# A norm's scale and offset both made on GpSimd, and the sample norm's parameter loads held until their tile's GELU, in an eight-core encoder trunk

## The chip, the cores and the metric

The kernel runs on all 8 cores of one Trainium2 chip. Each core works on its own part of the tokens and its span is measured on the device. The metric is the device time of the slowest core, in microseconds (us). The cores form two dies (cores 0 to 3 and cores 4 to 7).

Every execution lists the span of each core and its mean granted TensorE clock (1.0 is full speed). The program has two states. In the fast state all cores show a clock of about 0.996 and the program takes about 5100 us. In the slow state the cores of one die, sometimes of both, are granted less and the program takes from about 5190 to over 6000 us. The mean hides the form: on core 6 of the profiled run before, the clock was 0.81 from 25 to 385 us and 1.00 from 390 to 5130 us.

The rule that calls a run fast still lets in runs with a die at 0.986 to 0.991, which take 5136 to 5161 us. So I also quote "clean" runs: fast ones in which both dies have a clock (the median of their cores) of at least 0.995.

## The reference, cut to what matters

The model is a four-layer encoder trunk. Each layer is FFN, mixer, FFN, each with a residual and a LayerNorm. The change touches one norm inside the mixer, that of `v` in the spatial gating unit:

```python
# group B: gMLP spatial gating unit
z = jax.nn.gelu(h[..., 2 * D_CONV:], approximate=False)
u = z[..., :D_SGU]
v = layer_norm(z[..., D_SGU:], sgu_ln_g, sgu_ln_b)
s = u * sgu_mix(v, w_sgu, b_sgu)
# layer_norm: (x - mean) * rsqrt(var + 1e-5) * gain + offset, over the last axis (512 here)
...
return x, buf[:, -CONV_CTX:], v      # v of the sample streams is an output of its own
```

The normalised `v` of the sample streams (16 streams, 64 new frames each) is an output, so for these rows the kernel must also apply the norm's gain and offset explicitly. For all other rows they are folded into later operations.

## The kernel before: the parts that matter

The kernel writes down all operations of a half of the work with their dependencies and a planned duration (`dur`, in ns). A list scheduler (`schedule`) then simulates them and fixes in which order each engine issues them. Two consequences: a changed `dur` or dependency can reorder everything that comes after it, and an engine that waits at one entry of its list holds up all entries behind it.

A core does two halves; the sample rows sit in the last of three column groups of the second half. The norm of `v` handles up to four tiles of 128 tokens at once, so its statistics are arrays of 128 x 2 to 4 elements:

```python
def part_v(g, wv):
    ...
    for j, (v0, kk, t0, o0, on, smp) in enumerate(ts):
        op("pe", mm, ...)                                                   # L1018  v = x @ w_in
        op("act", ... activation(func=AF.Gelu) ..., kind="vg")              # L1023
        op("dve", ... bn_stats ..., kind="bn")                              # L1026
    ...                                                                     # L1031  bn_aggr: mean, variance
    Y, A = 36, 40
    op("dve", ... S(Y) = variance + EPS ..., dur=70)                        # L1040
    op("pool", ... S(Y) = S(Y) ** -0.5 ..., dur=900, port=True)             # L1042  scale
    op("dve", lambda e: e.scalar_tensor_tensor(out=S(A), in0=M2(0), scalar=-1.0, in1=S(Y),
              op0=ALU.mult, op1=ALU.mult), reads=[st], writes=[st], dur=70) # L1044  offset = -mean*scale
    for j, (...) in enumerate(ts):
        if not smp:
            op("act", ... activation(Identity, scale=Y[j], bias=A[j]) ...)  # L1054  v scaling (ScalarE)
            continue
        op("dve", ... (z - mean) * Y[j] ...)                                # L1059
        op("act", ... copy ...)                                             # L1063
        for hf in range(2):
            op("sp", ... dma_start(out=gb, in_=sgu_ln gain, broadcast to 128 partitions) ...)    # L1067
            op("sp", ... dma_start(out=be, in_=sgu_ln offset, broadcast to 128 partitions) ...)  # L1071
            op("dve", ... vo = z * gb ...)                                  # L1075
            op("pool", ... vo = vo + be ...)                                # L1078
            op("sp", ... dma_start(out=sgv_d[l], in_=vo) ...)
```

Everything issued with `"sp"` goes through one DMA queue, in list order. The same queue carries the shift copies of the depthwise convolution (L983 and L988), up to 32 per column group. They copy the convolution input into shifted positions, and the convolution's matmuls (L1119) need them:

```python
def part_a4(g):
    for s in range(4):
        for i in range(4):
            op("sp", ... dma_start(out=A4v[32*s:32*s+32, i, :, 0:wdt], in_=ABF[...]) ..., sem="a4")   # L983
            if smp:
                op("sp", ... dma_start(out=A4v[...], in_=ABF[...]) ..., sem="a4")                     # L988
```

Other lines in the profiles: L783 and L814 are the FFN's matmuls, L1177 the spatial mix (it reads the scaled `v`), L1230 the output projection, L604 the additions that prepare a LayerNorm's sums (on GpSimd and DVE), L654 and L677 the matmuls that finish those sums.

## Time and profile before

| | Time (us) | Note |
|---|---|---|
| 4 runs | 5103.65, 5105.04, 5728.84, 6049.52 | the first two fast, the others slow |
| Profiled run, a fifth | 5161.06 | called fast; die of cores 4 to 7 at 0.986 |
| Median of three | 5728.84 | a slow run |
| Core 2 in the profiled run | 5094.0 | clock 0.996 |
| Core 6 in the profiled run (slowest) | 5159.5 | clock 0.982 |

The page gives for each engine its busy time, its share of the span and its instructions. These are the engines of the slowest core before:

```profile
PE 5090.7 (99%) x34514; PEld 3093.9 (60%) x34514; DVE 2552.7 (49%) x5095; ACT 1850.6 (36%) x3513; POOL 1152.2 (22%) x1347
```

TensorE (PE) is busy 99% of the time. Nothing but TensorE work, its clock or its few waits can move the total; every other engine has slack on average. Core 6 had a lower clock in that execution, so from here on core 2 is read, which was undisturbed.

The list of TensorE's waits, core 2, before. Each line says which matmul waited, for which engine's or DMA's result, how long in all, how many times, and the longest:

```profile
PE psall L783 <- DMA ring<-w_all: 16.1, 1, 16.1
PE psall L1177 <- ACT ss L1054: 9.7, 5, 2.4
PE psall L677 <- DVE fr L675: 7.7, 4, 6.6
...
PE psall L1119 <- DMA sa<-abf: 1.5, 2, 0.8
```

The first line is the start of the kernel, when the first weights arrive. The second is what the change aims at: the spatial mix waits for the scaled `v`, up to 2.4 us at a time. The last: the convolution hardly waits for its shift copies.

The timeline of core 2 shows one of these waits (start, length, engine, line, operation, output<-input; in brackets the idle time of that engine before and what ended it):

```profile
3467.17 1.26 POOL L1042 TENSOR_TENSOR stat<-stat,nhalf 128x4 f32<-128x4 f32 x1
3468.42 0.99 POOL L604 TENSOR_TENSOR ss<-ss,X 128x384 f32<-128x384 f32 x1
3468.47 3.69 DVE L1044 SCALAR_TENSOR_TENSOR stat<-stat 128x4 f32<-128x4 f32 x1 [0.40 <-POOL stat L1042]
3469.38 0.98 POOL L604 TENSOR_TENSOR ss<-ss 128x384 f32<-128x384 f32 x1
3470.33 0.85 POOL L604 TENSOR_TENSOR ss<-ss,X 128x384 f32<-128x384 f32 x1
3471.15 0.98 POOL L604 TENSOR_TENSOR ss<-ss 128x384 f32<-128x384 f32 x1
3472.19 1.45 ACT L1054 ACTIVATE ss<-psall,stat 128x512 bf16<-128x512 f32 x2 [2.95 <-DVE stat L1044]
3474.91 0.43 PE L1177 MATMUL psall<-wt,ss 128*64 128x128 bf16 x6 [2.37 <-ACT ss L1054]
3476.98 3.99 PE L783 MATMUL psall<-XT,ring 128*128 128x384 bf16 x16
```

The offset takes 162 ns in the median of a core's 24 such instructions, which are of two to four columns. Here it takes 3.69 us, as do all four instructions of four columns on core 2. It begins within 0.05 us of the first of four back-to-back GpSimd additions and ends when the last of them ends. ScalarE has waited 2.95 us for it, and TensorE 2.37 us for ScalarE. The reason is in the table by windows (busy time of each engine, the granted clock, the DMA share and rate; core 2, before), of 20 us and of the dip inside them:

```profile
3472.00:3492.00 20.00, 17.64 (x121) 10.47 (x119) 16.44 (x38) 11.36 (x20) 15.50 (x16) 0.91 0.48 97
3476.10:3479.50 3.40, 3.40 (x20) 1.73 (x19) 2.63 (x8) 2.96 (x5) 3.40 (x4) 0.50 0.25 80
```

TensorE is busy all but the 2.36 us of its wait, but the clock granted over these 20 us is only 0.91: it falls to half for 3.41 us and is full otherwise. That is another 1.7 us (half of 3.41) that no list of waits shows.

### The profile page before, as it was taken

What the parts mean: (1) busy time and instruction counts of PE and PEld (TensorE: products, weight loads), DVE (VectorE), ACT (ScalarE), POOL (GpSimd) and SP (SyncE); (2) the same over time, 40 slices, a digit from 0 to 9 for tenths busy, and PEclk for the clock granted to TensorE, in tenths of its full rate; (3) what the DMA queues carried; (4) which work ended last, traced back from release to release, by engine and by line L of the source; (5) the groups of instructions that cost most, each with busy time, mean ns of one, the idle gap of its engine ahead of it and who ended that gap; (6) DMA issues with size and microseconds to landing.
All of it is one profiled execution on the core that took longest, in us unless ns stands there. A gap on an engine that the chain in (4) does not pass through costs nothing.

```text
span 5159.5 us, 86449 instructions; the slowest of 8 cores (5094.0 to 5159.5 us)
## 1 busy us (share of the span) xinstructions
PE 5090.7 (99%) x34514; PEld 3093.9 (60%) x34514; DVE 2552.7 (49%) x5095; ACT 1850.6 (36%) x3513; POOL 1152.2 (22%) x1347
## 2 busy tenths in 40 slices
PE   8999999999999999999999999999999999999998
PEld 4555666666666666666555555555555555555556
DVE  1267262672537553672527725267262682626736
ACT  1136131461326332461315513146131462313623
POOL 2014120141203311141202402015120151111410
PEclk8889999999999999999999999999999999999999
DMA  9334544345535545446834445344544445444451
GB/s 155 50 59 79 88 71 66 62 78 89 84 54 98 93 70 84 71 76 109 161 58 85 81 74 78 62 74 76 89 70 66 67 86 83 62 74 70 76 85 48
DMA packets 269208, 407.73 MB, mean 79 GB/s; under 512 B 33168, under 2 KB 107024, under 8 KB 268816
## 3 DMA queue, kind: packets, MB, share of 16 engines
q0 software_dynamic: 181360, 334.66, 41.6%
q1 hardware_dynamic: 87456, 67.54, 5.4%
q8 instruction: 284, 4.65, 0.4%
q14 instruction: 108, 0.88, 0.1%
HBM read 684.79 MB, written 11.47 MB: 135 GB/s over the span
## 4 chain that ended last, share of the span: by engine, by line
PE 94%; DVE 3%; ACT 1%; DMA 1%; SPq 1%; issue 0%; POOL 0%; ACTq 0%; DVEq 0%; POOLq 0%
PE psall L783 52%; PE psall L814 26%; PE psall L926 4%; PE psall L1230 3%; PE psall L1018 2%; PE psall L1119 2%; PE psall L1097 2%; SPq L983 1%; DVE X L726 1%; DVE ss L604 0%; DVE X L730 0%; DMA XT<-xin 0%; PE psall L1177 0%; PE psall L677 0%; PE psall L654 0%
## 5 line engine op out<-in xcount | busy, mean ns | idle before, releaser
L783 PE MATMUL psall<-XT,ring 128*128 128x384 bf16 (+3 forms) x16896 | 2757.8, 326 | 20.9 <-DMA ring<-w_all 18.2
L783 PEld LDWEIGHTS psall<-XT,ring 128*128 128x128 bf16 x16896 | 1657.8, 98 | 1105.1 <-issue 34.3
L789 ACT ACTIVATE ss<-psall 128x384 f32<-128x384 f32 (+3 forms) x1056 | 508.9, 484 | 1943.5 <-PE psall L783 1942.2
L814 PE MATMUL psall<-ss,ring 128*128 128x384 bf16 (+5 forms) x6272 | 1066.8, 323 | 0.0
L797 DVE TENSOR_TENSOR ss<-ss,psall 128x384 bf16<-128x384 f32 (+3 forms) x768 | 416.1, 547 | 1260.3 <-PE psall L783 1234.5
L585 POOL DMA_DIRECT2D ring<-w_all x623 | 449.3, 723 | 2312.6 <-PE psall L783 2019.1
L814 PEld LDWEIGHTS psall<-ss,ring 128*128 128x128 bf16 x6272 | 611.7, 98 | 382.8 <-issue 1.6
L613 ACT ACTIVATE ss<-X,sbi 128x384 f32<-128x384 f32 (+5 forms) x584 | 335.4, 600 | 700.7 <-DVE X L746 700.6
L746 DVE SCALAR_TENSOR_TENSOR X<-X,sg,psall 128x384 f32<-128x384 f32 (+5 forms) x584 | 342.3, 603 | 404.5 <-PE psall L814 394.7
L604 POOL TENSOR_TENSOR ss<-ss 128x384 f32<-128x384 f32 (+3 forms) x262 | 258.8, 988 | 1002.2 <-ACT ss L613 852.3
L797 DVE TENSOR_TENSOR sa<-ss,psall 128x384 bf16<-128x384 f32 (+3 forms) x288 | 157.7, 548 | 589.1 <-PE psall L783 589.1
L814 PE MATMUL psall<-sa,ring 128*128 128x384 bf16 (+5 forms) x2352 | 438.1, 323 | 0.0
L740 ACT ACTIVATE XT<-X,pars 128x384 bf16<-128x384 f32 (+3 forms) x528 | 320.1, 689 | 93.2 <-DVE X L730 93.0
L726 DVE SCALAR_TENSOR_TENSOR X<-X,sbi,psall 128x384 f32<-128x384 f32 (+5 forms) x584 | 333.6, 597 | 4.4 <-ACT ss L689 3.7
L814 PEld LDWEIGHTS psall<-sa,ring 128*128 128x128 bf16 x2352 | 230.5, 98 | 143.5
L604 DVE TENSOR_TENSOR ss<-ss 128x384 f32<-128x384 f32 (+5 forms) x393 | 239.9, 615 | 112.3 <-ACT ss L1133 64.6
L1230 PE MATMUL psall<-ss,ring 128*128 128x384 bf16 (+3 forms) x1536 | 253.3, 324 | 6.6 <-ACT ss L1158 5.7
L926 PE MATMUL psall<-XT,ring 128*128 128x384 bf16 (+4 forms) x1536 | 257.9, 327 | 0.1
L730 DVE TENSOR_TENSOR X<-X,psall 128x384 f32<-128x384 f32 (+4 forms) x512 | 237.4, 543 | 0.1
L1230 PEld LDWEIGHTS psall<-ss,ring 128*128 128x128 bf16 x1536 | 148.1, 98 | 105.9 <-issue 16.9
L926 PEld LDWEIGHTS psall<-XT,ring 128*128 128x128 bf16 x1536 | 149.1, 98 | 100.2 <-issue 1.5
L699 ACT ACTIVATE ss<-ss 128x384 f32<-128x384 f32 (+4 forms) x194 | 99.3, 512 | 221.9 <-DVE ss L694 113.5
(115 smaller groups left out, 2933.8 us busy)
## 6 DMA issues: line engine op xcount, KB each, us to landing
ring<-w_all POOLq DMA_DIRECT2D x623, 512.0 KB, 7.0
sa<-abf SPq DMA_DIRECT2D x204, 103.0 KB, 2.3
sa<-abf SPq DMA_DIRECT2D x68, 102.8 KB, 2.4
X<-xin SPq DMA_DIRECT2D x4, 1536.0 KB, 32.3
y<-X SPq DMA_DIRECT2D x8, 768.0 KB, 9.3
sa<-abf SPq DMA_DIRECT2D x60, 78.5 KB, 2.2
X<-xin SPq DMA_DIRECT2D x2, 1656.0 KB, 21.8
XT<-xin POOLq DMA_DIRECT2D x4, 768.0 KB, 17.7
```

The costliest lines, as they stand in the source:

```text
L585: op("pool", lambda e: e.dma_start(out=RING[t.slot][:].rearrange("p (h n) -> p h n", h=2), in_=w_d[u].rearrange("h p n -> p h n")), writes ...
L604: op(eng, lambda e: e.tensor_tensor(out=self.sa(o), in0=a[0](), in1=b[0](), op=ALU.add), reads=[a[1], b[1]], writes=[o], dur=d_pool(n) if ...
L613: op("act", lambda e: e.activation(out=self.sa(sq), in_=src(), func=AF.Square, **kw), reads=rd, writes=[sq], dur=d_act(n, 1 if sqb is not ...
L726: op("dve", lambda e, k=k: e.scalar_tensor_tensor(out=xs(k), in0=xs(k), scalar=SBI[:, q, k:k + 1], in1=PS[:, m.slot, 0:n], op0=ALU.add, op ...
L740: op("act", lambda e, k=k: e.activation(out=XT[:, k, c0:c1], in_=xs(k), func=AF.Identity, scale=lg[:, k:k + 1], bias=lb[:, k:k + 1]), read ...
L746: op("dve", lambda e: e.scalar_tensor_tensor(out=X[:, k, c0:c1], in0=X[:, k, c0:c1], scalar=SG[:, q, k:k + 1], in1=PS[:, bank.slot, 0:n], ...
L783: ins = e.matmul(PS[:, bank.slot, 0:n], lhsT=RING[w.slot][:, h * 1024 + k * 128:h * 1024 + (k + 1) * 128], rhs=XT[:, k, c0:c1], start=(k = ...
L789: op("act", lambda e, bg=bg, sil=sil, n=n: e.activation(out=SS[sil.slot][:, 0:n], in_=PS[:, bg.slot, 0:n], func=AF.Silu), reads=[bg], writ ...
L797: return e.tensor_tensor(out=gap(gts)[:, o0:o0 + n], in0=SS[sil.slot][:, 0:n], in1=PS[:, bu.slot, 0:n], op=ALU.mult)
L814: ins = e.matmul(PS[:, y.slot, 0:n], lhsT=RING[wd[b // 16].slot][:, (b % 16) * 128:(b % 16 + 1) * 128], rhs=gap(gt[g][f // 2])[:, o0:o0 + ...
L926: ins = e.matmul(PS[:, bank.slot, 0:n], lhsT=RING[wa[c].slot][:, h * 1024 + k * 128:h * 1024 + (k + 1) * 128], rhs=XT[:, k, c0:c1], start= ...
L1230: ins = e.matmul(PS[:, y.slot, 0:n], lhsT=RING[wo[d // 2].slot][:, o0:o0 + 128], rhs=SS[src.slot][:].bitcast(BF16)[:, (k % 2) * GW:(k % 2) ...
```

## The change

The intent is twofold. The offset moves to GpSimd, right behind the scale, so that the chain loses one crossing between engines and the stalled DVE instruction disappears. And the gain and offset loads of the sample norm wait for their tile's GELU, so that they do not occupy work buffers for most of a layer.

```diff
+                    vgi.append(len(G.ops) - 1)           # the GELU of tile j
 ...
-                op("dve", ... S(Y) = variance + EPS ..., dur=70)
+                def ynm(e):
+                    e.tensor_scalar(out=S(Y), in0=M2(1), scalar1=EPS, scalar2=None, op0=ALU.add)
+                    return e.tensor_scalar(out=S(NM), in0=M2(0), scalar1=-1.0, scalar2=None, op0=ALU.mult)
+                ynm.multi = True
+                op("dve", ynm, reads=[st], writes=[st], dur=140)
                 op("pool", lambda e: e.tensor_tensor(out=S(Y), in0=S(Y), in1=NHALF[:, 0:nt], op=ALU.pow),
-                   reads=[st, tONE], writes=[st], dur=900, port=True)
-                op("dve", lambda e: e.scalar_tensor_tensor(out=S(A), in0=M2(0), scalar=-1.0, in1=S(Y), op0=ALU.mult,
-                                                           op1=ALU.mult), reads=[st], writes=[st], dur=70)
+                   reads=[st, tONE], writes=[st], dur=1200, port=True)
+                op("pool", lambda e: e.tensor_tensor(out=S(A), in0=S(NM), in1=S(Y), op=ALU.mult), reads=[st], writes=[st],
+                   dur=150, port=True)
 ...
                            writes=[be], dur=650, dma=400, sem="sgb%d%d" % (l, hf))
+                        for o in G.ops[-2:]:             # the gain load and the offset load
+                            o.after.add(vgi[j])
```

More of the change, by code (lines that the diff above doesn't have):

```diff
@@ L1010, in part_v @@
                 st = Tile("st", "st")
-                vbs, zs = [], []
+                vbs, zs, vgi = [], [], []
                 for j, (v0, kk, t0, o0, on, smp) in enumerate(ts):
@@ L1036, in S @@
                     return STAT[st.slot][:, a:a + b]
-                Y, A = 36, 40
+                Y, A, NM = 36, 40, 44
                 def M2(b):
                     return STAT[st.slot][:, 24:24 + 2 * nt].rearrange("p (a b) -> p a b", b=2)[:, :, b]
-                op("dve", lambda e: e.tensor_scalar(out=S(Y), in0=M2(1), scalar1=EPS, scalar2=None, op0=ALU.add),
-                   reads=[st], writes=[st], dur=70)
+                def ynm(e):
[3 more added lines that the diff above has]
+                op("dve", ynm, reads=[st], writes=[st], dur=140)
                 op("pool", lambda e: e.tensor_tensor(out=S(Y), in0=S(Y), in1=NHALF[:, 0:nt], op=ALU.pow),
-                   reads=[st, tONE], writes=[st], dur=900, port=True)
-                op("dve", lambda e: e.scalar_tensor_tensor(out=S(A), in0=M2(0), scalar=-1.0, in1=S(Y), op0=ALU.mult,
-                                                           op1=ALU.mult), reads=[st], writes=[st], dur=70)
+                   reads=[st, tONE], writes=[st], dur=1200, port=True)
+                op("pool", lambda e: e.tensor_tensor(out=S(A), in0=S(NM), in1=S(Y), op=ALU.mult), reads=[st], writes=[st],
+                   dur=150, port=True)
                 for j, (v0, kk, t0, o0, on, smp) in enumerate(ts):
```

## The prediction

> **What bounds the kernel.** TensorE. The page's first part gives it 5090.7 us busy of a 5159.5 us span (99%), the chain of work that ended last is 94% TensorE, and the cores' list shows granted clocks of 0.98 to 1.00. By stretches, TensorE idles 19 us before 30 us, 18.5 us after 5130 us, and only 31 us (0.6%) in between; that is all there is to win.
>
> **What the change removes, adds and moves.**
> - DVE: out goes the scalar_tensor_tensor for the offset, 24 times, median 162 ns; in comes a tensor_scalar of the same size.
> - GpSimd: 24 more multiplications on 2 to 4 elements. The pow on the same tiles takes 876 ns and a 256-column addition 732 ns; my estimate from these is 0.2 to 0.5 us each, on an engine 22% busy.
> - One crossing between engines goes: DVE, GpSimd, DVE, ScalarE becomes DVE, GpSimd, ScalarE.
> - The eight gain and eight offset loads of the sample norm move. The timeline of the DMA queue shows them running far ahead: three at 2 to 3 us, used at 2881 us; the others at 2711, 3367, 4025 and 4684 us. So three or four of the 30 work buffers are held nearly throughout.
>
> **How much is critical.** In the list of waits TensorE waits for the v norm's scaling 4 times, 7.3 us in all, 2.2 us the longest. The timeline shows why: in the second half's layers 1 to 3 the small offset instruction on DVE takes 3.7 us instead of 0.16, and ends just as four back-to-back GpSimd additions end. The Trainium skill, "SBUF — State Buffer", section "SBUF: two separate sides", says that a DVE instruction with two SBUF inputs and a GpSimd one exclude each other for a whole instruction; this trace agrees (3.69 to 3.70 us, three times). The new GpSimd multiplication at worst queues behind one 1 us addition. I expect 5 to 7 us from it.
>
> The parameter loads: DVE needs them about 20 us after the GELU, and they land in 3.4 us, so nobody should wait. Four issues of 0.43 us may fall among the 32 shift copies of the last group and push these by up to 2 us per layer (TensorE waits for such copies 4.1 us now). The freed buffers matter little: hardly any TensorE wait is for buffers. The order is recomputed from changed durations, so other waits will shift by some us.
>
> **Prediction.** The ratio of fast runs is 0.999: 5098 us in the fast state against 5103.65, with 5075 to 5125 for fast runs alone. A median of three may be a slow run, as 5728.84 was; the recorded range, 5075 to 5760, allows for that, not for an effect of the change. Chances on fast runs: faster by over 2% 0.02, within 2% 0.96, slower 0.02.
>
> **What would show it.** The 3.7 us DVE instruction is gone; TensorE's wait for the v scaling falls from 7.3 to under 2 us; GpSimd gains 24 short instructions; the parameter loads sit at about 2855, 3515, 4170 and 4830 us; TensorE's busy time is unchanged within 0.5% at equal clock.
>
> **What would make it wrong.** The new order starves the shift copies or a LayerNorm chain, so that TensorE's idle time grows by more than 20 us; parameter loads arrive late and hold up DVE; a difference of clock is taken for one of the change.

## The result, and the profile after

Ratios here are the mean time of one kernel's fast runs over that of the other's fast runs of the same rounds, so they are not quite the ratio of the medians that I quote.

| | Fast runs (us) | Slow runs (us) |
|---|---|---|
| before | 5103.65, 5105.04 | 5728.84, 6049.52 |
| after | 5099.83, 5099.93, 5100.05, 5100.81 | 5430.03 |

The ratio of fast runs is 0.9992, 95% interval 0.9968 to 1.0016: no change. The medians over all runs (5100.37 after, 5416.94 before, of four each) differ by 6%, and this says only how many slow runs each kernel happened to get.

The engines on the page of the kernel after (its slowest core was core 2):

```profile
PE 5025.7 (99%) x34514; PEld 3074.9 (60%) x34514; DVE 2554.9 (50%) x5095; ACT 1849.0 (36%) x3513; POOL 1152.1 (23%) x1371
```

GpSimd has 24 instructions more (1371 against 1347), as it should. TensorE's busy time on core 2 is 5025.7 us; on the same core before it was 5024.2. So the work is the same; the waits have been exchanged. The list of TensorE's waits, core 2, after (lines from L1045 on are shifted by up to 8: L1127 is the convolution, L1185 the spatial mix):

```profile
PE psall L783 <- DMA ring<-w_all: 14.9, 1, 14.9
PE psall L654 <- DVE fr L645: 9.7, 8, 4.7
PE psall L1127 <- DMA sa<-abf: 7.8, 6, 3.7
PE psall L677 <- DVE fr L675: 7.7, 4, 6.6
```

The 9.7 us wait of the spatial mix is gone. In its place stand 7.8 us for the shift copies (1.5 before) and 9.7 us for the DVE half of a LayerNorm (L645; 1.3 before). The same place in the timeline of core 2, after:

```profile
3466.44 1.03 POOL L1048 TENSOR_TENSOR stat<-stat,nhalf 128x4 f32<-128x4 f32 x1 [9.18 <-DVE stat L1045]
3468.06 2.80 POOL L733 TENSOR_TENSOR X<-X,ss 128x384 f32<-128x384 f32 x3 [0.59 <-ACT ss L708]
3470.82 0.20 POOL L1050 TENSOR_TENSOR stat<-stat 128x4 f32<-128x4 f32 x1
3475.04 0.76 ACT L1060 ACTIVATE ss<-psall,stat 128x512 bf16<-128x512 f32 x1
3479.48 0.43 PE L1185 MATMUL psall<-wt,ss 128*64 128x128 bf16 x6
```

The new multiplication (L1050) takes 0.20 us. It stands behind three instructions of a LayerNorm, 2.80 us, which the scheduler placed between it and its pow. The spatial mix no longer waits: its line has no bracket. And this is what the DMA queue does around one of the sample groups, after (SPq is the issue on the queue; L1073 and L1077 are the parameter loads, L983 and L988 the shift copies):

```profile
2798.68 1.06 SPq L983 DMA_DIRECT2D sa<-abf  x1
2799.78 0.60 SPq L988 DMA_DIRECT2D sa<-abf  x1
2800.51 0.51 SPq L1073 DMA_DIRECT2D ss<-sgu_ln  x1
2801.12 0.37 SPq L1077 DMA_DIRECT2D ss<-sgu_ln  x1
2801.89 0.33 SPq L1073 DMA_DIRECT2D ss<-sgu_ln  x1
2802.33 0.37 SPq L1077 DMA_DIRECT2D ss<-sgu_ln  x1
2802.74 0.59 SPq L983 DMA_DIRECT2D sa<-abf  x1
2803.38 0.61 SPq L988 DMA_DIRECT2D sa<-abf  x1
2806.85 1.16 PE L1127 MATMUL psall<-sa,dw 128*32 128x286 bf16 x32 [0.97 <-DMA sa<-abf]
```

The four loads go out between the last two pairs of shift copies. They put off the issue of the last pair by about 2.3 us (the L988 ahead of them ends at 2800.38, the next L983 begins at 2802.74), and the convolution waits for exactly that pair: by the trace its last copy lands at 2806.60. Before, these loads were issued long in advance (the first three at 2 to 3 us into the kernel).

### The profile page after: what moved, and what is told of

Its sections match the earlier page's. It is cut to its first block, busy times and chain, and to the rows that moved or that the text cites. A ratio compares the mean times of both kernels' runs of the same rounds, so it can differ in the third digit from the quotient of the medians.

```text
span 5098.2 us, 86121 instructions; the slowest of 8 cores (5087.5 to 5098.2 us)
## 1 busy us (share of the span) xinstructions
PE 5025.7 (99%) x34514; PEld 3074.9 (60%) x34514; DVE 2554.9 (50%) x5095; ACT 1849.0 (36%) x3513; POOL 1152.1 (23%) x1371
## 4 chain that ended last, share of the span: by engine, by line
PE 91%; DVE 5%; SPq 1%; ACT 1%; DMA 1%; issue 0%; POOL 0%; ACTq 0%; DVEq 0%; POOLq 0%
PE psall L783 52%; PE psall L814 26%; PE psall L926 4%; PE psall L1238 3%; PE psall L1127 2%; PE psall L1018 2%; PE psall L1105 1%; DVE X L726 1%; SPq L983 1%; DVE ss L604 0%; DVE X L746 0%; DMA sa<-abf 0%; DVE X L730 0%; DMA XT<-xin 0%; SPq L988 0%
## 5 line engine op out<-in xcount | busy, mean ns | idle before, releaser
L783 PE MATMUL psall<-XT,ring 128*128 128x384 bf16 (+3 forms) x16896 | 2716.1, 323 | 20.4 <-DMA ring<-w_all 14.9
L814 PE MATMUL psall<-ss,ring 128*128 128x384 bf16 (+5 forms) x6272 | 1053.1, 320 | 0.0
L604 DVE TENSOR_TENSOR ss<-ss 128x384 f32<-128x384 f32 (+5 forms) x393 | 253.7, 652 | 112.9 <-ACT ss L1141 63.1
```

The costliest lines, as they stand in the source:

```text
L604: op(eng, lambda e: e.tensor_tensor(out=self.sa(o), in0=a[0](), in1=b[0](), op=ALU.add), reads=[a[1], b[1]], writes=[o], dur=d_pool(n) if ...
L783: ins = e.matmul(PS[:, bank.slot, 0:n], lhsT=RING[w.slot][:, h * 1024 + k * 128:h * 1024 + (k + 1) * 128], rhs=XT[:, k, c0:c1], start=(k = ...
L814: ins = e.matmul(PS[:, y.slot, 0:n], lhsT=RING[wd[b // 16].slot][:, (b % 16) * 128:(b % 16 + 1) * 128], rhs=gap(gt[g][f // 2])[:, o0:o0 + ...
```

## The experiments

The theory after this reading (call it **two real effects**): the norm part gains the v waits and more, and the load part loses about as much through the shift copies. The rivals: **nothing happened** (the v wait had slack behind it and the new waits are those that always come next); **the order** (both parts are harmless, but the recomputed list order moves waits about at random); and **the start** (the removed early loads speed up the first tiles).

To separate the order from the parts, some kernels keep the list order of the kernel before: the schedule is computed with the old operations and then one operation is exchanged or moved in the finished list. These are called "fixed order" below. All kernels gave correct results.

The table sums up the clean runs; each is read in its place below. "Before" is the kernel before in the same job on the same chip.

| Run | Norm | Loads | Order | Clean median (n) | Before, clean median (n) | Ratio of fast runs [95%] |
|---|---|---|---|---|---|---|
| e1_norm_only | new | old | recomputed | 5100.19 (5) | 5099.06 (5) | 0.9987 [0.9946, 1.0028] |
| e2_loads_only | old | new | recomputed | 5115.10 (5) | 5099.06 (5) | 1.0014 [0.9973, 1.0056] |
| e3_norm_fixed_order | new | old | before's | 5088.16 (4) | 5099.06 (5) | 0.9963 [0.9915, 1.001] |
| e4_late_first_loads | old | first three later | before's | 5098.93 (4) | 5099.06 (5) | 0.9982 [0.9925, 1.0039] |
| e5_both_fixed_order | new | first three later | before's | 5086.68 (6) | 5100.46 (5) | 0.996 [0.9931, 0.9989] |
| e6_change_again | new | new | the change's | 5099.81 (1) | 5100.46 (5) | none |
| e7_loads_behind_copies | new | behind the copies | the change's | 5093.15 (2) | 5100.46 (5) | 0.9973 [0.9916, 1.0031] |
| e8_offset_one_input | DVE, one input | old | before's | 5089.60 (4) | 5100.46 (5) | 0.9966 [0.9929, 1.0003] |
| e9_plan_only | old, pow planned at 1200 | old | recomputed | 5120.81 (3) | 5102.38 (3) | 1.0003 [0.9934, 1.0071] |
| e10_loads_fixed_order | old | new | before's | none | 5102.38 (3) | none |
| e11_change_fixed_order | new | new | before's | 5101.09 (2) | 5102.38 (3) | 0.9993 [0.9907, 1.0078] |
| e12_fixed_behind_copies | new | behind the copies | before's | none | none | none |
| e13_behind_copies_again | new | behind the copies | before's | 5084.52 (4) | 5099.57 (6) | 0.9969 [0.9953, 0.9986] |
| e14_fixed_before_last_copies | new | new | before's | 5100.83 (4) | 5099.57 (6) | 1.0002 [0.9987, 1.0017] |

e11 and e14 are the same kernel, and so are e12 and e13. Where the clean medians and the ratio disagree (e2, e9), fast runs of the kernel before with a die at 0.986 to 0.991 (5136 to 5154 us) are the reason. With them several intervals include 1; those of e5 and e13 do not.

### e1_norm_only: the norm part alone

The edit is the change without its last two lines:

```diff
-                        for o in G.ops[-2:]:
-                            o.after.add(vgi[j])
```

> Only the norm part of the change (GpSimd makes scale and offset); the parameter loads stay free to run ahead; the list order is computed anew. Theory (the waits are real and separate): TensorE's wait for the v norm's scaling goes from 7 to 10 us per core to under 1 us; the first matmul still starts at about 18 us, since three parameter loads still go out at 2 to 3 us; no parameter load stands among the shift copies, so TensorE's wait for copies stays at 2 to 4 us; whole time 5094 to 5102 us, depending on what the new order costs elsewhere. Rival (one wait only hands over to the next): the v wait goes, and waits for the LayerNorm sums grow by the same 7 to 9 us; 5103 to 5105 us.

It took 5100.19 us, the kernel before 5099.06: nothing gained, although the stalled DVE instruction is gone. The list of TensorE's waits, core 2, shows what came instead:

```profile
PE psall L783 <- ACT XT L740: 8.6, 2, 8.1
```

One FFN matmul now waits 8.1 us for a LayerNorm's output. That wait is in no other kernel here; it comes from the recomputed order, not from the norm. So a part of a change cannot be judged in a kernel whose whole order was recomputed for it.

### e2_loads_only: the load part alone

The edit is the kernel before plus `vgi` and the two `after` lines.

> Only the load part of the change (parameter loads of the sample norm not before their tile's GELU in the order); the norm is as before. Theory: the first matmul starts 2 to 4 us earlier (about 15 instead of 18 us), because 3 times 128 KB no longer compete with the first tiles; the v wait stays at 7 to 10 us; in the second half TensorE waits 1 to 2 us per layer more for the last shift copies, because four loads of 0.4 us stand among them; together 5100 to 5105 us. Rival (loads don't matter to anybody): start, waits and time as before within 1 us.

It took 5115.10 us (5114.54 to 5115.55) against 5099.06: 16 us slower. TensorE's waits, core 2:

```profile
PE psall L1233 <- ACT ss L1161: 20.1, 7, 3.3
...
PE psall L1122 <- DMA sa<-abf: 10.5, 7, 4.4
```

The waits for shift copies went from 1.5 to 10.5 us, which is the load part's own mark. The waits of the output projection went from 6.0 us to 20.1, in four places of 3.3 us; these come with the order. So of the 16 us this run cannot say how much is the loads.

### e3_norm_fixed_order: the norm part, with the order of before

```diff
         order = schedule(G, ...)                      # computed with the old operations
+        for ipow, ioff, f in offs:                    # f: GpSimd tensor_tensor, NM * Y
+            G.ops[ioff].eng, G.ops[ioff].fn = "pool", f
+            order.remove(ioff)
+            order.insert(order.index(ipow) + 1, ioff)
```

> The norm part alone with the order of before held fixed on every engine: only the offset moves from DVE to GpSimd, right behind the pow. Theory: the v wait (7 to 10 us) goes and nothing else moves, 5094 to 5097 us (8 us less than before). Rival (one wait hands over to the next): the v wait goes and waits for the LayerNorm sums right after it grow by as much; 5102 to 5105 us.

It took 5088.16 us (5086.19 to 5092.16), 10.9 us less than the kernel before, and the ranges do not overlap (before: 5097.02 to 5102.25). The timeline of core 2 at the place that was shown above:

```profile
3462.17 1.27 POOL L1047 TENSOR_TENSOR stat<-stat,nhalf 128x4 f32<-128x4 f32 x1
3463.58 0.20 POOL L1052 TENSOR_TENSOR stat<-stat 128x4 f32<-128x4 f32 x1
3463.74 0.99 POOL L605 TENSOR_TENSOR ss<-ss,X 128x384 f32<-128x384 f32 x1
3464.16 1.43 ACT L1061 ACTIVATE ss<-psall,stat 128x512 bf16<-128x512 f32 x2
3467.72 0.43 PE L1184 MATMUL psall<-wt,ss 128*64 128x128 bf16 x6
3469.52 2.77 PE L784 MATMUL psall<-XT,ring 128*128 128x384 bf16 x16
```

The four additions still follow (the first is shown), but the offset is done before they begin. The spatial mix does not wait, and the next 16 FFN matmuls take 2.77 us instead of 3.99. The table by windows, core 2, says why:

```profile
3465.00:3485.00 20.00, 20.00 (x144) 12.20 (x142) 18.75 (x38) 10.99 (x20) 16.57 (x18) 1.00 0.60 119
```

TensorE is busy 20.00 of 20 us at a clock of 1.00. With the wait went the dip of the clock that followed it. The trace of core 2 has six such dips before and two in e3, each of 3.41 us at half clock, so of 1.7 us (the first 20 us and a longer low clock at the very end left out). Of the four that are gone, three followed v waits; the fourth, at 1598.7 us, followed a LayerNorm wait of 1.2 us and is still there in e8, so it is not put down to the norm. So the gain of core 2 has two terms, 9.0 us of v waits (9.7 less 0.7 that stay) and 5.1 us of clock. They sum to 14.1, and its span fell by 15.0 us (5094.0 to 5079.0; the two come from different jobs). One core in one run is a rough measure: in clean runs of the kernel before the span of core 2 goes from 5086.4 to 5100.7 us. The mean over all cores and clean runs fell by 12.1 us (5093.4 to 5081.3), the slowest core by 10.9.

The Trainium skill, "TensorE: Matmul & The Clock Gate", section "HAM oscillation — how this bites in real kernels", gives the rule to avoid TensorE gaps of more than about 3.4 us. Here gaps of 2.1 to 2.4 us (the v waits) were followed by a reduced clock at three of the four places on core 2, so the measurement decides: the gaps that cost clock can be shorter than the page's figure.

### e4_late_first_loads: the three loads at the start

The edit moves only the three parameter loads issued at 2 to 3 us to a later place (by the traces they go out at about 365 us):

```diff
+        early = [...the three sgg/sgb loads in order[:400]...]
+        for i in early: order.remove(i)
+        k = order.index(kc1) + 1                      # behind the second load of convolution weights
+        order[k:k] = early
```

> Before with one thing changed: the three parameter loads that went out at 2 to 3 us go out about 430 us later, with the same buffers and the same order of all else. Theory: the first matmul starts 2 to 4 us earlier, and everything after it moves by that: 5100 to 5102 us. Rival (the start's scatter between cores has other causes): start at 16 to 19 us as before, 5103 to 5105 us.

It took 5098.93 us against 5099.06: nothing. The first matmul does start earlier. By the list of TensorE's waits, the first matmuls wait for their weights (on core 3, for one, 14.2 in e4 and 19.2 before). Over the cores they wait 14.2 to 15.4 us in e4, 16.1 to 19.2 us before, and 14.3 to 15.9 us in the change. So the start is real but reaches the slowest core's time in none of the runs. Where it is lost is open: on core 1 some of it reappears as longer idle time of the convolution near 985 us (4.3 against 1.9 us, of the 4.3 only 2.6 for shift copies), which one trace is not enough to establish. The rival "the start" falls as an explanation of the total.

### e5_both_fixed_order: e3 and e4 together

The edit is that of e3 plus that of e4.

> The order of before held fixed; the offset on GpSimd behind the pow, and the three first parameter loads 430 us later. Theory: 5085 to 5090 us, the 11 us of the norm alone in the fixed order, and 0 to 3 us more from the earlier start, since the earlier start alone did not shorten the slowest core. Rival (the earlier start adds fully): 5083 to 5085 us. It should be 10 us faster than the change itself on the same chip.

It took 5086.68 us (5083.65 to 5088.2) against 5100.46 (5098.67 to 5101.17), 13.8 us less; ratio 0.996, interval 0.9931 to 0.9989. It repeats e3's gain on another chip. The 3 us beyond e3's 10.9 are within what jobs differ by, so they are not evidence for the early loads.

### e6_change_again: the change on another chip

The kernel is the change, unedited, as the companion for e5 and e7.

> The change as given, once more, so that it stands beside the others on one chip: 5099 to 5101 us, within 3 us of before.

Only one of eight runs was clean, 5099.81 us; the rest were slow. Over all runs, the clean one with both its dies, the slowest core of an undisturbed die took 5095.1 to 5101.4 us (9 dies). It agrees with the first result. Its waits for shift copies on core 2 were

```profile
PE psall L1127 <- DMA sa<-abf: 8.2, 6, 2.3
```

### e7_loads_behind_copies: the change, its loads behind the last copy

```diff
         order = schedule(G, ...)                      # the change's own order
+        # per layer: move the parameter loads that stand ahead of the group's last "a4" copy to right behind it
```

> The change with its own order held fixed, except that the four parameter loads per layer go behind the last shift copies of that group instead of before their last pair. Theory (the loads delay the copies): in the second half TensorE's wait for shift copies falls from 0.7 to 1.5 us per layer to under 0.3 us, the time by 3 to 5 us to 5095 to 5098 us; the parameters still land over 5 us before they are read. Rival (the copies are late for another reason, the order of TensorE's own work): the waits stay, 5099 to 5101 us.

Two clean runs took 5093.02 and 5093.27 us, 6.7 less than the change in the same job; ten undisturbed dies gave 5090.0 to 5092.1 us, below all nine of e6. The waits for shift copies on core 2 (the profile is of a slow run, but core 2's die was undisturbed, at 0.997) fell to

```profile
PE psall L1127 <- DMA sa<-abf: 4.6, 3, 2.7
```

So within the change, moving nothing but the place of these loads on the queue gives back about 7 us. "Nothing happened" falls with this: the load part does cost time.

### e8_offset_one_input: is it the second input from SBUF?

Here the offset stays on DVE, at its old place in the old order, but each instruction reads one tensor and takes the scale as a per-partition scalar:

```diff
-                op("dve", ... scalar_tensor_tensor(out=S(A), in0=M2(0), scalar=-1.0, in1=S(Y), ...))
+                for j in range(nt):
+                    r = e.tensor_scalar(out=A[j], in0=mean[j], scalar1=Y[j], scalar2=-1.0,
+                                        op0=ALU.mult, op1=ALU.mult)
```

> The order of before, the offset stays on DVE, but as one tensor_scalar per tile with a single tensor operand and the scale as its per-partition scalar, instead of one instruction with two tensors. Theory (the long instruction waits for SBUF ports that GpSimd's back-to-back additions hold, because it reads two tensors from SBUF): the 3.7 us instructions are gone, each takes about 0.2 us, the v wait falls from 7 to 10 us to under 2 us, 5087 to 5093 us. Rival 1 (the crossing from GpSimd back to DVE is what costs): the stall stays at 3 to 4 us and the time at 5097 to 5102 us. Rival 2 (any DVE instruction that works in SBUF alone is held off): the stall stays too, with the first of the tensor_scalars taking it.

It took 5089.60 us (5087.54 to 5090.66), 10.9 us less than before, as e3 did. The timeline of core 2:

```profile
3466.51 0.99 POOL L604 TENSOR_TENSOR ss<-ss,X 128x384 f32<-128x384 f32 x1
3466.64 0.58 DVE L1046 TENSOR_SCALAR stat<-stat 128x1 f32<-128x1 f32 x4 [0.46 <-POOL stat L1042]
```

The four DVE instructions run at the same time as the first GpSimd addition and take 0.58 us together. The Trainium skill, "SBUF — State Buffer", section "Who interferes with whom", says that a DVE instruction with two SBUF inputs contends with a GpSimd instruction that reads SBUF, and that one with at most one SBUF input does not (outside two modes that use both ports). This pair of runs agrees: 3.69 us with two inputs, 0.58 us for all four with one, in the same order. That the gain is the same as e3's also shows that GpSimd is not needed for it: both forms of the offset that do not wait for the additions gain the same.

### e9_plan_only: nothing but the plan

```diff
-                   reads=[st, tONE], writes=[st], dur=900, port=True)
+                   reads=[st, tONE], writes=[st], dur=1200, port=True)
```

> Before with one number changed in the plan, none in any instruction: the scheduler believes that the pow takes 1200 ns instead of 900, as the change lets it. So the same instructions run in a new order. Theory (the recomputed order is what gave the gain back): the time moves by up to 12 us either way, with waits of LayerNorm chains in the first half at other places and of other sizes; the 3.7 us DVE instruction may come or go with the order. Rival (a new order costs nothing by itself): within 2 us of before.

No instruction is different, only the scheduler's idea of how long the pow takes. The three clean runs took 5120.77 to 5121.24 us against 5101.41 to 5104.1: 18 us slower. TensorE's waits, core 2:

```profile
PE psall L1230 <- POOL ss L1213: 25.1, 3, 8.4
```

In three layers the output projection waits 8.4 us for a gate's addition on GpSimd. So the rival "the order" is a real effect too, and as large as the others. A recomputed order alone moved the time by 18 us here, with no instruction changed. It is why e1 and e2 are not added up here.

### e10_loads_fixed_order: the load part, with the order of before

```diff
+        for ia, ib, ig in lds[::-1]:                  # gain load, offset load, their tile's GELU
+            order.remove(ia); order.remove(ib)
+            k = order.index(ig) + 1
+            order[k:k] = [ia, ib]
```

> The order of before held fixed, only the sixteen parameter loads go right behind their tile's GELU in it, which puts them before the last pair of shift copies of each layer of the second half. Theory (loads cost through the copies, and alone little): the v wait stays at 7 to 10 us, waits for copies rise by 2 to 6 us, the first matmul starts up to 4 us earlier; 5098 to 5104 us, and not the 15 us more of the load part with a recomputed order. Rival (the late loads themselves cost the 15 us): 5110 to 5116 us.

None of its 11 runs was fast, so there is no time to quote beside the others. In those where one die was undisturbed, that die's slowest core took 5104.7 to 5112.3 us, median 5109.4 (7 dies); the kernel before in the same job, by the same measure, 5097.3 to 5102.6, median 5099.1 (13 dies). That is about 10 us slower, by a weaker measure. The waits, core 2 (undisturbed, at 0.996):

```profile
PE psall L1122 <- DMA sa<-abf: 13.9, 7, 3.4
PE psall L1180 <- ACT ss L1056: 9.5, 5, 2.4
```

The v wait is as before (9.5 against 9.7 us), and the waits for copies are 13.9 instead of 1.5 us.

### e11_change_fixed_order: both parts, with the order of before

The edit is that of e3 plus that of e10.

> The whole change with the order of before held fixed: offset on GpSimd behind the pow, loads behind their GELU. Theory: the gain of the norm part (11 us) less the cost of the loads through the copies (2 to 6 us): 5088 to 5095 us, that is 5 to 12 us faster than the change with its own recomputed order. Rival (the change costs something that no order cures): 5098 to 5101 us.

Two clean runs took 5100.79 and 5101.40 us, the kernel before 5102.38 in the same job. That is the figure of the rival, not of the theory: also without any change of order, both parts together give nothing. The v wait is gone, and the convolution waits 14.7 us for the copies on core 2. (That profile was of a run of 5145.23 us with a die at 0.990; its core 2 is read only for the kind of wait.)

### e12_fixed_behind_copies: an inconclusive run

The kernel is e11 with the loads placed behind the last shift copy:

```diff
-            k = order.index(ig) + 1
+            k = max(k for k, i in enumerate(order) if k < rd and G.ops[i].sem == "a4") + 1   # rd: first reader
```

> The whole change in the fixed order of before, as in the run before this (which took 5101 us against 5088 us without the loads' move), but the four parameter loads per layer go behind the last pair of shift copies instead of before it. Theory (the 13 us are the last copies' delay and nothing else): TensorE's wait for shift copies in the second half falls from about 2.0 to 2.8 us per layer to under 0.5 us, and the time to 5085 to 5090 us, as far below before as the norm alone was. Rival (the loads' bytes, or their late arrival at DVE, cost by themselves): 5095 to 5101 us.

That chip gave no clean run: eight runs took 5193 to 16029 us (in the longest, one core had a mean clock of 0.355) and the kernel before had no clean one in eleven. The shortest is called fast by the rule, with dies at 0.980 and 0.972. So its time says nothing. The waits for copies on cores 0 to 3 (at 0.991 to 0.994) were 4.3, 2.1, 4.7 and 1.9 us, against 16.5, 11.5, 14.7 and 9.9 in e11.

### e13_behind_copies_again and e14_fixed_before_last_copies: one difference only

e13 is the kernel of e12 and e14 that of e11. Between the two, only the place of 16 loads in one queue's list differs.

> The same kernel as the run before, whose chip gave no undisturbed die: the whole change in the fixed order of before, parameter loads behind the last shift copies. Theory (the loads cost only by delaying the copies): 5085 to 5090 us in the fast state. Rival (bytes or late arrival of the loads cost too): 5095 to 5101 us.

> The partner of the run beside it on the same chip: the whole change in the fixed order of before, parameter loads ahead of the last pair of shift copies. Theory: 10 to 15 us more than its partner, 5099 to 5102 us in the fast state, all of it waits for shift copies. Rival: no difference between the two.

On the same chip in the same job, e13 took 5084.52 us (5082.75 to 5086.56), e14 5100.83 (5098.68 to 5102.08) and the kernel before 5099.57 (5097.6 to 5101.87). So the place of the loads is worth 16 us, and e13 beats the kernel before by 15 us or 0.3%; its ratio to it is 0.9969, interval 0.9953 to 0.9986. The waits for copies on core 2 in e14:

```profile
PE psall L1129 <- DMA sa<-abf: 14.3, 6, 3.0
```

and in e13:

```profile
PE psall L1129 <- DMA sa<-abf: 3.3, 3, 1.6
```

The timeline of core 2 in e14 shows a batch of 32 convolution matmuls after such a wait, in two layers:

```profile
3455.58 1.16 PE L1129 MATMUL psall<-sa,dw 128*32 128x286 bf16 x32 [3.02 <-DMA sa<-abf]
...
4112.84 2.10 PE L1129 MATMUL psall<-sa,dw 128*32 128x286 bf16 x32 [2.72 <-DMA sa<-abf]
```

and in e13 the batch of the second of these layers:

```profile
4104.21 1.16 PE L1129 MATMUL psall<-sa,dw 128*32 128x286 bf16 x32
```

In the second layer of e14 the same 32 matmuls took 2.10 us: the clock had fallen again, 0.91 over the window from 4105 to 4125 us. In the first it had not, after an even longer wait. The traces show a pattern behind the difference. All dips of a core start on one grid of 3.413 us, to 0.01 us (on core 2, before, the starts at 2179.0 and 3476.1 us are 380 steps apart), and a dip goes with how little TensorE was busy in the grid interval just before. On core 2 in e14 it was busy 0.94 of the 3.41 us before the dip at 4112.6, while the wait of 3.02 us lies across two intervals of 2.06 and 1.73 us busy. A count over all cores without a 0.81 stretch, 104 in 15 of the kept traces (the first and last 30 us left out), says: each of the 322 intervals under 40% busy was followed by a dip, none over 70% was, and in between both occur. So the same wait can cost 1.7 us more or nothing, by where it falls. Of the 15.2 us by which core 2's span differs between the two (5094.9 and 5079.7), 11.0 us are waits for copies, and the rest is matmuls that took longer: the convolution's are busy 125.0 us in e14 and 123.0 in e13, the output projection's 253.9 and 251.6.

The Trainium skill, "DMA: Bandwidth & Descriptors", section "Issuing engines are not separate DMA queues", says that issuing from several engines saves only the sequencer's time to initiate a DMA, usually small beside the DMA itself. Here too the issue is the smaller part of one DMA (about 0.6 us, and a copy lands 2.3 us after its issue begins), but in one queue the issues add up: 32 of them in a row are about 19 us (an estimate, 32 x 0.6). Four more entries ahead of the last pair put off its issue by 2.1 us (in e14, 4106.30 to 4108.37). That is not all. The last pair also lands later after its issue when the loads are just ahead of it. The last copies of that layer, KB and us from issue to landing, in e14:

```profile
sa<-abf SPq DMA_DIRECT2D x1, 46.2 KB, 3.6
```

and in e13 (two copies of this size):

```profile
sa<-abf SPq DMA_DIRECT2D x2, 46.2 KB, 2.1
```

In the four layers the last copy lands after 3.0 to 3.6 us in e14 and after 2.1 us in e13. So about two thirds of the delay is place in the queue and one third, 0.9 to 1.5 us, goes with the loads' own transfers of 128 KB each; no run separates the two.

### What adds up

With the order held fixed, starting from the kernel before (each from clean medians of one job): the norm part gives -10.9 us (e3, and e8 by another route). Adding the loads to it brings the total to -1.3 us in e11 and to +1.3 in e14, so the loads cost about 10 to 12 us. Placing them behind the copies brings it to -15.1 (e13), so against e13 they cost 16. e13 and e5, which both lack the three early loads, lie 3 to 4 us below e3 and e8; whether the earlier start adds something to the norm part stays open. In the change's own order the loads cost 6.7 us (e6 and e7, one and two clean runs); the norm's gain less this would leave 4 us, and the clean runs of the change show between 0.7 us (e6) and about 4 us (the first result, mean against mean; the clocks of its two runs before are not on record). So what is left for the change's own new order is between 0 and 4 us, and cannot be resolved further.

Several expectations missed in size: e2 (5100 to 5105 us expected, 5115 measured), e3 (5094 to 5097, 5088), e9 (up to 12 us, 18), e10 (5098 to 5104, about 5109 by its weaker measure) and e11 (5088 to 5095, 5101). And of e14's excess not all is waits for copies, as was expected, but 11.0 of 15.2 us on core 2.

## Why the prediction was right or wrong

The effect on fast runs was as predicted: a ratio of 0.999 against 0.9992 measured. The reasons were only partly so, and the agreement is luck.

- **The step that failed.** It is the sum of the two parts. 5103.65 less 5 to 7 us for the norm is the 5098; the loads' delay of the shift copies was named ("by up to 2 us per layer") and then booked at zero. Both terms were mis-sized: the norm part measured 10.9 us (e3, e8), and the loads cost 6.7 us in the change's order (e6 against e7) and 10 to 16 us in the order of before (e11, e14 against e3, e13). The errors have opposite signs and nearly cancel.
- **The time itself.** The prediction put 5098 us, a time of the fast state, beside a kernel whose quoted median, 5728.84 us, was a slow run, and its range up to 5760 covered both states. Read as a ratio to that median, 5098 claims an 11% gain; the medians over all runs showed 6%, and neither has to do with the change. The prediction knew this and said so ("a median of three may be a slow run"), but one number cannot stand for two states. The fast runs after (median 5099.99) agree with the 5098.
- **The stalled DVE instruction.** Right. 3.7 us through four GpSimd additions, a cost of having two SBUF inputs: e8 takes the second input away and the stall with it.
- **Its worth, "5 to 7 us".** Too small. It measured 10.9 us (e3, e8). The estimate took the 7.3 us of waits of the page's core and shaved it; core 2 had 9.7, and the term left out is the clock, which fell to half for 3.41 us after three of the four longer waits on core 2, 1.7 us each time.
- **The new multiplication, "0.2 to 0.5 us", "at worst behind one 1 us addition".** The duration was right (0.19 to 0.21 us). The worst case was wrong: it stood behind three LayerNorm instructions, 2.80 us. That cost nothing, because in the change's order the spatial mix comes 12.0 us after the end of the pow (before: 6.5 us, its wait included).
- **"Nobody should wait" for the parameters.** Right for the parameters themselves: DVE was not held up. The issue was their effect on others, and there the prediction named the mechanism, "may push these by up to 2 us per layer", and then booked nothing for it in the sum. The waits for copies in the fixed order were up to 3.0 us in a layer, with clock on top. The prediction counted only the four issues of 0.43 us; the later landing of the last pair (3.0 to 3.6 instead of 2.1 us) was missing.
- **"Other waits will shift by some us".** The mechanism was right and the size was too small: e9 shows 18 us from a planned duration alone.
- **The start.** Not predicted: the first matmul begins up to 5 us earlier (e4). It is not seen in the total; why is open.
- **The marks in the profile.** The loads were expected at about 2855, 3515, 4170 and 4830 us and came at about 2800, 3450, 4110 and 4770, so some 60 us earlier, between the last two pairs of their group's shift copies. The 24 instructions and TensorE's busy time came as predicted.

So the small total was predicted for a partly wrong reason: not one small gain, but a gain of 11 us and a loss of nearly the same, of which 7 us are the loads and the rest is not resolved.

## What to carry to other kernels

When a kernel is at 99% of one engine, a change that "does nothing" may be two effects that cancel: test the parts separately, and hold the computed order fixed, because reordering alone was worth up to 18 us here. On a DMA queue it is the place in the list that counts: a small load that nobody waits for still costs what it delays, so put it behind the entries that something does wait for. And a short TensorE wait costs more than its length when the clock drops after it: read the granted clock of the window that follows, and expect the loss to come and go with small shifts in time.

The best kernel (e13) takes both parts of the change, keeps the old order, and issues the loads behind the last shift copies; it is 15 us faster than the kernel before in the same job, and as much below the clean runs of the change in other jobs.

## What the Trainium skill lacked or had wrong

- "SBUF — State Buffer": it says that the loser of the shared port is blocked for the whole instruction of the other. It does not say that a blocked DVE instruction can lose to a whole train of back-to-back GpSimd instructions: 3.69 us, through four of 0.85 to 0.99 us.
- "TensorE: Matmul & The Clock Gate": it warns of idle gaps over about 3.4 us. Here gaps of 2.1 to 3.0 us were often, not always, followed by half clock for 3.41 us (1.7 us lost; 16 matmuls in 3.99 instead of 2.77 us). It has no figure for a stretch that is only partly idle: here 322 of 322 grid intervals of 3.41 us under 40% busy were followed by a dip, and none over 70% busy.
- The same page, section "Seeing it yourself", advises to budget 13/16 of the clock for sustained dense matmuls on all cores. Here eight cores, each 99% busy with matmuls for 5.1 ms, ran at 0.994 to 0.998 in every clean run. The slow state, in about half the runs, is in the kept traces that clock for a part of the time: 0.81 from 25 to 385 us on core 6, before, then 1.00 with the same work going on.
- "DMA: Bandwidth & Descriptors": issue time is called usually small beside the DMA itself. That holds for one DMA here (0.3 to 0.6 of 2 to 4 us), but no figure says how issues add up in one queue: four loads at the wrong place, with the later landing behind them, cost TensorE 2.7 to 3.0 us in a layer (e14).
- No page that I found gives the time of very small GpSimd instructions: on 128 x 2 to 4 elements a multiplication took 0.19 to 0.21 us and a pow 0.71 to 1.27 us.
